# Seven-product pairs of the up projection: sums by accumulation in PSUM, and 19 pairs instead of 16

## The chip, the cores and the metric

The kernel runs on one core of one Trainium2 chip. The metric is the device time of one execution in microseconds (us); lower is better. Six engines matter here: TensorE (PE in the profile, with its weight loads as PEld), VectorE (DVE), ScalarE (ACT), GpSimd (POOL) and the DMA queues, of which SyncE (SP) issues most.

## What is computed

The reference is one decoder layer on 512 tokens of width 1024: adaLN modulation, a token mixer, a residual with LayerNorm, then a convolutional gated MLP and a second residual with LayerNorm. Only the MLP is touched:

```
def conv_ffn(h, w_up, conv_w, conv_b, w_down):
    u = causal_dwconv(h @ w_up, conv_w, conv_b)
    g, val = jnp.split(u, 2, axis=-1)
    return (jax.nn.silu(g) * val) @ w_down
```

`w_up` is 1024 x 5632 (g and val, 2816 columns each), `w_down` 2816 x 1024, all float32. The depthwise convolution has three taps along the tokens.

## The kernel before

Every float32 operand is split into a high and a low part of the type fp32r, and a product is three matmuls (high by high, high by low, low by high; `mm3`, line 456). Splitting is a copy by ScalarE (the high part, `wh` or the first half of `wq`) and a subtraction by VectorE (the low part).

The up projection has 22 pairs: pair j is 128 columns of g and the 128 columns of val that are multiplied with them. A plain pair is two tiles of 8 row chunks of 128: 2 x 8 x 3 = 48 matmuls of 128x128 weights by 512 tokens, into two banks of PSUM. Pairs 0 and 1 run in two halves of the tokens. A pair in the list `SEVEN` (line 695) is computed in Winograd's form of Strassen's scheme: the pair's weights (g and val columns, rows 0 to 511 and 512 to 1023) and the activations (the same rows, tokens 0 to 255 and 256 to 511) are 2 x 2 blocks, and seven products of sums of blocks take the place of eight. Each product is 4 chunks x 3 = 12 matmuls by 256 tokens, so a pair is 84.

- `sums_seven` (line 716) forms two sums of weight blocks by DMA: one load by SP and two accumulating DMAs by POOL per pair.
- `split_seven` (line 764) forms two more sums on VectorE (`sw`) and splits the seven left operands into `wq`: seven copies on ScalarE, seven subtractions on VectorE.
- `quarters` (line 1318) forms and splits four sums of activation blocks, `ts`, once.
- `seven` (line 1660) issues the products 0, 1, 2, 4, 5, 6, 3 into four banks, `sP`. `seven_out` (line 1692) combines them: two ScalarE copies to SBUF (`m1`) and seven VectorE additions of 256 columns.
- `up_post` (line 1358) then does, for each of the two tiles, the convolution: one ScalarE pass and two VectorE passes (`conv3`); after that a Silu, the product of the two tiles, and for j below 6 the split of the result (`mid`); the others are kept and split later.

The down projection (`dn`) follows, 122.76 us of TensorE.

The order of instructions is written by a planner in the kernel's own code (class `Order`): coroutines offer their next operation, the planner prices it, keeps a clock per engine, and issues what could start first, by priority among those close together. Once written, the order is fixed: each engine takes its instructions in that order and waits by semaphores. Pools bound what may be ahead: 8 banks of PSUM, 9 buffers `s` (2 KB a partition: `sw`, `m1`, `u2`, `u`), 10 buffers for split weights in this stage. In the trace all operations have line 309, where the planner issues them; they are told apart by tiles.

Of the kernel before, what the change touches and what calls it, by code (L numbers as in the profile page):

```python
# [11 lines left out]
AF = mybir.ActivationFunctionType  # L12
# [4 lines left out]
P = 128  # L17
# [396 lines left out]
def layer_kernel(  # L414
# [21 lines left out]
    R = Order(nc)  # L436
    T, V, A, G, S, GD = (Engine(R, k) for k in ("PE", "V", "A", "G", "S", "GD"))
# [15 lines left out]
    def row_bc(src, off, n):  # L453
        return bass.AP(tensor=src.tensor, offset=src.offset + off, ap=[[0, P], [1, n]])

    def mm3(ps, lh, ll, rh, rl, start, stop):
        return [T.matmul(ps, lh, rh, start=start, stop=False),
                T.matmul(ps, lh, rl, start=False, stop=False),
                T.matmul(ps, ll, rh, start=False, stop=stop)]

    def bank(group, name="ps", after=()):
        return Alloc("ps", [P, 512], F32, name, group, after)

    def buf(cls, shape, name, group=None, dt=F32):
        return Alloc(cls, shape, dt, name, group)
# [226 lines left out]
            rows_item(w_out, k, n)  # L692
    UP0 = len(items)
    NSPLIT = 4
    SEVEN = [3, 5, 6, 7, 8, 10, 11, 12, 13, 15, 16, 17, 18, 19, 20, 21]
    for j, i in up_tiles:
        cols_item(w_up, i * D_FF + j * P)
    for n in range(2):
# [4 lines left out]
    def w_load():  # L703
        yield Need("loads")
        for i, (shape, src) in enumerate(items):
# [4 lines left out]
            j = (i - UP0) // 2  # L710
            if i == UP0 + 2 * j + 1 and j in SEVEN:
                R.spawn(sums_seven(j, raw, items[i - 1][1][:, :4], src[:, :4]), 4)
# [3 lines left out]
    def sums_seven(j, r1, a11, a21):  # L716

        q = yield buf("s", [P, 4, P], "sw")
        yield S.dma_start(q, a11)
        yield GD.dma_start(r1[:, :4], r1[:, 4:], accum_op=OP.add)  # L720
        yield GD.dma_start(q, a21, accum_op=OP.add)
        QS[j] = q
        R.mark(("qs", j))

    def w_split():
        yield Need(("hk", KC - 1))
        for i, (shape, _) in enumerate(items):
# [6 lines left out]
            if 0 <= i - len(items) + LATE_DN < 2:  # L734
                yield Need("fin")
                m = 2 * (i - len(items) + LATE_DN)
                hi, lo = RES["w"][:, m], RES["w"][:, m + 1]
            elif UP0 <= i < UP0 + 2 * NFF and (i - UP0) // 2 in SEVEN:
                if (i - UP0) % 2 == 0:
# [24 lines left out]
    def split_seven(j, r0, r1):  # L764

        yield Need(("qs", j))
        a11, a12, s1, a22, s3 = r0[:, :4], r0[:, 4:], r1[:, :4], r1[:, 4:], QS.pop(j)
        dst, src, tmp = {}, {0: a11, 1: s1, 4: s3, 5: a12, 6: a22}, {}

        def make(m, x, y):  # L770
            t = tmp[m] = yield buf("s", [P, 4, P], "sw")
            yield V.tensor_add(t, x, y)
            src[m] = t

        def hi(m):
            dst[m] = yield buf("b", [P, 2, 4, P], "wq", "w2", F32R)
            yield A.activation(dst[m][:, 0], src[m], AF.Copy)

        def lo(m):
            q = [dst[m][:, 1], src[m], dst[m][:, 0].bitcast(F32)]  # L780
            yield V.tensor_sub(*q)
            WS[j, m] = dst[m]
            lead[1] += 2 / 7
            R.mark(("ws", j, m))

        yield from hi(0)
        yield from hi(1)
        yield from make(2, s1, a11)
        yield from lo(0)
        yield from lo(1)  # L790
        yield from hi(2)
        yield from lo(2)
        yield from hi(4)
        yield from make(3, src[2], a12)
        R.free(tmp[2])
        yield from lo(4)
        R.free(s3)
        for m in (5, 6, 3):
            yield from hi(m)
            yield from lo(m)  # L800
        R.free(tmp[3])

    def w_next():
        i = wpos[0]
        wpos[0] += 1
        if not (UP0 <= i < UP0 + 2 * NFF and (i - UP0) // 2 in SEVEN):
            lead[0] += 1
        R.mark(("item", i))
        return ("w", i), i
# [541 lines left out]
    def conv3(ps, dst, ch, neg):  # L1351
        f0, f1, f2 = (nfw[:, i, ch - NFF:ch - NFF + 1] if neg else w[:, ch:ch + 1] for i, w in enumerate((fw0, fw1, fw2)))
        yield A.activation(dst, ps, AF.Identity, bias=fb[:, ch:ch + 1], scale=f2)
        for s, fw in ((1, f1), (2, f0)):
            yield V.scalar_tensor_tensor(dst[:, s:], ps[:, :SEQ - s], fw, dst[:, s:], op0=OP.mult, op1=OP.add)
        R.free(ps)

    def up_post(j, i, ps, neg=False):
        u = yield buf("s", [P, SEQ], "u")
        yield from conv3(ps, u, j + 22 * i, neg)  # L1360
        if i == 0:
            yield A.activation(u, u, AF.Silu)
            U[j] = u
            R.mark(("u", j))
            return
        yield Need(("u", j))
        g = U.pop(j)
        if j >= NMID:
            if not 12 <= j < 20 and j % 2 == 0:
                KEEP[j] = yield buf("b", [P, 2, SEQ], "keep", "mid")  # L1370
                R.mark(("keep", j))
            n = 4 if 12 <= j < 20 else 2
            yield Need(("keep", j - j % n))
            k = KEPT[j] = KEEP[j - j % n][:, j % n]
            yield V.tensor_mul(k, g, u)
            R.free(g, u)
            R.mark(("kept", j))
            return
        yield V.tensor_mul(g, g, u)
        R.free(u)  # L1380
        mid = yield buf("b", [P, 2, SEQ], "mid", "mid", F32R)
        yield A.activation(mid[:, 0], g, AF.Copy)
        yield V.tensor_sub(mid[:, 1], g, mid[:, 0].bitcast(F32))
        R.free(g)
        MID[j] = mid
        R.mark(("mid", j))
# [109 lines left out]
    def products():  # L1496
# [37 lines left out]
        for kind, i in G1:  # L1534
            if kind == "v":
# [3 lines left out]
                for k0 in range(0, KC, 2):  # L1539
                    key, n = w_next()  # L1540
                    yield Need(key)
                    hi, lo = W.pop(n)
                    for kk in range(2):
                        k = k0 + kk
                        for t in range(NT):
                            yield mm3(ps[t], hh[:, k, t * P:(t + 1) * P], hl[:, k, t * P:(t + 1) * P],
                                      hi[:, kk], lo[:, kk], k == 0, k == KC - 1)
                    R.free(hi, lo)
# [3 lines left out]
            else:  # L1552
# [4 lines left out]
                for k in range(KC):  # L1557
                    yield mm3(ps, w[0][:, k], w[1][:, k], hh[:, k], hl[:, k], k == 0, k == KC - 1)
# [99 lines left out]
    L, H = slice(0, 256), slice(256, 512)  # L1658

    def seven(j):  # L1660

        h2h, h2l = H2["hl"]
        for _ in range(2):
            w_next()
        ps = []
        for i in range(2):
            ps.append((yield bank("gemm", "sP")))

        def b(k0, c):
            return h2h[:, k0:k0 + 4, c], h2l[:, k0:k0 + 4, c]  # L1670

        def t(m):
            return TS[m][:, 0], TS[m][:, 1]

        yield Need("ts")
        R.mark("tsused")

        for m, p, c, (rh, rl) in ((0, 0, L, b(0, L)), (1, 1, L, t(0)), (2, 0, H, t(1)), (4, 1, H, t(2)),
                                  (5, 2, L, b(4, L)), (6, 3, L, t(3)), (3, 2, H, b(4, H))):
            if p == len(ps):  # L1680
                ps.append((yield bank("gemm", "sP")))
            yield Need(("ws", j, m))
            w = WS.pop((j, m))
            lead[0] += 2 / 7
            for k in range(4):
                yield mm3(ps[p][:, c], w[:, 0, k], w[:, 1, k], rh[:, k], rl[:, k], k == 0, k == 3)
            R.free(w)
            if m == 0:
                R.spawn(seven_out(j, ps), 2)
            R.mark(("sm", j, m))  # L1690

    def seven_out(j, ps):
        m1 = yield buf("s", [P, 2, 256], "m1")
        yield A.activation(m1[:, 0], ps[0][:, L], AF.Copy)
        yield Need(("sm", j, 1))
        yield A.activation(m1[:, 1], ps[1][:, L], AF.Copy)
        yield Need(("sm", j, 2))
        u2 = yield buf("s", [P, 2, 256], "u2")
        yield V.tensor_add(u2[:, 0], ps[0][:, H], m1[:, 0])
        R.free(ps[0])  # L1700
        yield Need(("sm", j, 4))
        yield V.tensor_add(u2[:, 1], ps[1][:, H], u2[:, 0])
        R.free(ps[1])
        yield Need(("sm", j, 5))
        yield V.tensor_add(ps[2][:, L], ps[2][:, L], m1[:, 0])
        yield V.tensor_add(u2[:, 0], u2[:, 0], m1[:, 1])
        yield Need(("sm", j, 6))
        yield V.tensor_add(ps[3][:, L], ps[3][:, L], u2[:, 1])
        yield V.tensor_add(ps[3][:, H], u2[:, 1], m1[:, 1])
        R.free(m1)  # L1710
        R.spawn(up_post(j, 1, ps[3], True), 2)
        yield Need(("sm", j, 3))
        yield V.tensor_add(ps[2][:, H], ps[2][:, H], u2[:, 0])
        R.free(u2)
        R.spawn(up_post(j, 0, ps[2]), 2)

    def ffn():
        h2h, h2l = H2["hl"]
# [21 lines left out]
        for n, (j, i) in enumerate(up_tiles[NSPLIT:]):  # L1740
            if j in SEVEN:
                if i == 0:
# [115 lines left out]
```

## Time and profile before

| | |
|---|---|
| median of 3 runs | 704.72 us (703.95 to 705.64) |
| profiled execution | 704.55 us, span 702.5 us |
| PE busy | 688.8 us of the span (98%) |
| DVE busy | 621.0 us (88%) |
| ACT busy | 367.0 us (52%) |
| granted TensorE clock, mean | 0.997 |
| up projection, first to last matmul | 343.9 to 572.3 us |
| down projection on PE | 572.28 us, for 122.76 us |

Busy time is the time in which at least one instruction of the engine is running; instructions of an engine overlap somewhat, so the distance between the starts of successive instructions is often shorter than the duration shown. An idle time has the name of what ended it. A granted clock of 1.00 is 2.4 GHz.

### The profile page before, as it was taken

What the parts mean: (1) busy time and instruction counts of PE and PEld (TensorE: products, weight loads), DVE (VectorE), ACT (ScalarE), POOL (GpSimd) and SP (SyncE); (2) the same over time, 40 slices, a digit from 0 to 9 for tenths busy, and PEclk for the clock granted to TensorE, in tenths of its full rate; (3) what the DMA queues carried; (4) which work ended last, traced back from release to release, by engine and by line L of the source; (5) the groups of instructions that cost most, each with busy time, mean ns of one, the idle gap of its engine ahead of it and who ended that gap; (6) DMA issues with size and microseconds to landing.
All of it is one profiled execution on the core that took longest, in us unless ns stands there. A gap on an engine that the chain in (4) does not pass through costs nothing.

```text
span 702.5 us, 11338 instructions
## 1 busy us (share of the span) xinstructions
PE 688.8 (98%) x4197; PEld 595.4 (85%) x4197; DVE 621.0 (88%) x1172; ACT 367.0 (52%) x680; POOL 97.2 (14%) x103
## 2 busy tenths in 40 slices
PE   8999999999999999999999999999999999999995
PEld 7787777888888888887898899899899998888885
DVE  5889989899999999889999999999999999567646
ACT  2447568846677454223886556656655676211300
POOL 0010021101000000000111112112111100960023
PEclk9999999999999999999999999999999999999998
DMA  8997074143455727776576466766777574432202
GB/s 268 315 281 249 5 235 127 37 117 98 122 182 169 235 68 253 254 265 216 171 184 141 109 162 166 150 162 176 142 193 154 136 248 167 156 103 76 91 30 91
DMA packets 131322, 114.25 MB, mean 163 GB/s; under 512 B 4421, under 2 KB 110273, under 8 KB 131267
## 3 DMA queue, kind: packets, MB, share of 16 engines
q1 hardware_dynamic: 120515, 105.14, 48.4%
q0 software_dynamic: 10752, 8.39, 8.4%
q8 instruction: 33, 0.54, 0.3%
q14 instruction: 22, 0.18, 0.1%
HBM read 105.09 MB, written 4.23 MB: 156 GB/s over the span
## 4 chain that ended last, share of the span: by engine, by line
PE 83%; DVE 8%; DMA 3%; SPq 3%; issue 1%; ACT 1%; POOL 0%; DVEq 0%; ACTq 0%; POOLq 0%
PE sP L309 20%; PE fm L309 18%; PE dn L309 17%; PE po L309 7%; PE up L309 6%; PE first L309 3%; SPq L309 3%; PE tm L309 2%; DVE u L309 2%; DVE wq L309 2%; PE psS L309 2%; PE pov L309 1%; PE pT L309 1%; PE py L309 1%; DMA csb<-drcs 1%
## 5 line engine op out<-in xcount | busy, mean ns | idle before, releaser
L309 DVE TENSOR_TENSOR wl<-raw,wh 128x1024 fp32r<-128x1024 f32 x70 | 87.2, 1250 | 25.8 <-ACT wh L309 25.6
L309 ACT ACTIVATE wh<-raw 128x1024 fp32r<-128x1024 f32 x70 | 73.4, 1054 | 69.1 <-DVE raw L309 23.3
L309 PE MATMUL dn<-wh,mid 128*128 128x512 f32 (+1 forms) x356 | 102.6, 371 | 0.0
L309 PE MATMUL sP<-ts,wq 128*128 128x256 f32 x768 | 96.1, 281 | 0.0
L309 PEld LDWEIGHTS sP<-ts,wq 128*128 128x128 f32 x768 | 92.9, 188 | 0.2 <-ACT m L309 0.2
L309 PEld LDWEIGHTS dn<-wh,mid 128*128 128x128 f32 x356 | 64.6, 188 | 12.6
L309 PE MATMUL sP<-h2h,wq 128*128 128x256 f32 x384 | 74.4, 282 | 0.0
L309 PE MATMUL fm<-hh,wh 128*128 128x512 f32 x176 | 72.6, 412 | 0.0
L309 PE MATMUL fm<-hh,wl 128*128 128x512 f32 x176 | 69.4, 394 | 0.0
L309 PE MATMUL fm<-hl,wh 128*128 128x512 f32 x176 | 69.4, 394 | 0.0
L309 PE MATMUL dn<-wl,mid 128*128 128x512 f32 (+1 forms) x178 | 66.1, 371 | 0.0
L309 PEld LDWEIGHTS sP<-h2h,wq 128*128 128x128 f32 x384 | 61.6, 189 | 0.5 <-DVE sP L309 0.3
L309 PE MATMUL sP<-h2l,wq 128*128 128x256 f32 x192 | 53.9, 281 | 0.0
L309 DVE TENSOR_TENSOR wq<-raw,wq 128x512 fp32r<-128x512 f32 x64 | 43.1, 685 | 0.2
L309 PE MATMUL up<-h2h,wh 128*128 128x256 f32 (+1 forms) x128 | 43.2, 338 | 0.0
L309 PE MATMUL up<-h2l,wh 128*128 128x256 f32 (+1 forms) x128 | 43.2, 337 | 0.0
L309 PE MATMUL up<-h2h,wl 128*128 128x256 f32 (+1 forms) x128 | 43.1, 337 | 0.0
L309 PE MATMUL po<-wh,os 128*128 128x512 f32 x128 | 42.1, 396 | 0.0
L309 PEld LDWEIGHTS fm<-hh,wl 128*128 128x128 f32 x176 | 33.1, 188 | 7.7
L309 ACT ACTIVATE wq<-raw 128x512 fp32r<-128x512 f32 x64 | 37.6, 621 | 3.6 <-DVE u L309 2.1
L309 PEld LDWEIGHTS fm<-hh,wh 128*128 128x128 f32 x176 | 33.2, 188 | 7.1 <-issue 0.7
L309 PEld LDWEIGHTS dn<-wl,mid 128*128 128x128 f32 x178 | 33.5, 188 | 6.2
(268 smaller groups left out, 1540.5 us busy)
## 6 DMA issues: line engine op xcount, KB each, us to landing
raw<-in_ffn_up_w_dram SPq DMA_DIRECT2D x44, 512.0 KB, 3.9
raw<-in_mix_in_w_dram SPq DMA_DIRECT2D x26, 512.0 KB, 5.5
ad<-in_ada_w_dram SPq DMA_DIRECT2D x24, 512.0 KB, 4.0
raw<-in_ffn_down_w_dram SPq DMA_DIRECT2D x22, 512.0 KB, 4.1
aw<-in_ada_w_dram SPq DMA_DIRECT2D x32, 256.0 KB, 5.8
raw<-in_mix_out_w_dram SPq DMA_DIRECT2D x12, 512.0 KB, 4.0
csb<-drcs SPq DMA_DIRECT2D x8, 512.0 KB
ad<-in_ada_w_dram SPq DMA_DIRECT2D x4, 1024.0 KB
```

The lines of the kernel that those rows point to most:

```text
L309: getattr(self.hw[op.eng], op.fn)(*op.args, **op.kw)
```

## The change

`SEVEN` now holds the pairs 3 to 21, 19 of them; pair 2 alone remains plain, and pairs 4, 9 and 14 pass from plain to seven products. Within a pair, products are added up in PSUM where their sum is wanted: product 0 opens an accumulation in the left half of the first bank, products 2, 4 and 6 go on in it, and product 3 goes on in product 1's half of the second bank. Because other results need the partial sums, ScalarE copies the half to SBUF (`c1`, `c2`) after products 0, 2, 1 and 4; products 2, 4, 3 and 6 start only after the copy of what they add to (`Need(("sc", j, after))`). Two VectorE additions are left of seven, one of 512 columns and one of 256. A pair takes two banks instead of four. The products run in the order 0, 5, 2, 1, 4, 3, 6, and the weights are split in the order 0, 5, 2, 1, 4, 3, 6. `seven_out` has priority 1 instead of 2.

```diff
-    SEVEN = [3, 5, 6, 7, 8, 10, 11, 12, 13, 15, 16, 17, 18, 19, 20, 21]
+    SEVEN = list(range(3, 22))
...
         yield from hi(0)
-        yield from hi(1)
+        yield from hi(5)
         yield from make(2, s1, a11)
         yield from lo(0)
-        yield from lo(1)
+        yield from lo(5)
         yield from hi(2)
         yield from lo(2)
-        yield from hi(4)
+        yield from hi(1)
         yield from make(3, src[2], a12)
         R.free(tmp[2])
-        yield from lo(4)
-        R.free(s3)
-        for m in (5, 6, 3):
+        yield from lo(1)
+        for m in (4, 3, 6):
...
-        for m, p, c, (rh, rl) in ((0, 0, L, b(0, L)), (1, 1, L, t(0)), (2, 0, H, t(1)), (4, 1, H, t(2)),
-                                  (5, 2, L, b(4, L)), (6, 3, L, t(3)), (3, 2, H, b(4, H))):
-            if p == len(ps):
-                ps.append((yield bank("gemm", "sP")))
+        for m, p, c, (rh, rl), after, go_on in ((0, 0, L, b(0, L), None, True), (5, 1, L, b(4, L), None, False),
+                                                (2, 0, L, t(1), 0, True), (1, 1, H, t(0), None, True),
+                                                (4, 0, L, t(2), 2, True), (3, 1, H, b(4, H), 1, False),
+                                                (6, 0, L, t(3), 4, False)):
+            if after is not None:
+                yield Need(("sc", j, after))
...
-                yield mm3(ps[p][:, c], w[:, 0, k], w[:, 1, k], rh[:, k], rl[:, k], k == 0, k == 3)
+                yield mm3(ps[p][:, c], w[:, 0, k], w[:, 1, k], rh[:, k], rl[:, k],
+                          k == 0 and after is None, k == 3 and not go_on, p == 0 or m in (1, 3))
...
     def seven_out(j, ps):
-        m1 = yield buf("s", [P, 2, 256], "m1")
-        yield A.activation(m1[:, 0], ps[0][:, L], AF.Copy)
...
+        c1 = yield buf("s", [P, 2, 256], "c1")
+        yield A.activation(c1[:, 0], ps[0][:, L], AF.Copy)
+        R.mark(("sc", j, 0))
+        c2 = yield buf("s", [P, 2, 256], "c2")
+        yield Need(("sm", j, 2))
+        yield A.activation(c1[:, 1], ps[0][:, L], AF.Copy)
+        R.mark(("sc", j, 2))
+        yield Need(("sm", j, 1))
+        yield A.activation(c2[:, 0], ps[1][:, H], AF.Copy)
+        R.mark(("sc", j, 1))
         yield Need(("sm", j, 4))
+        yield A.activation(c2[:, 1], ps[0][:, L], AF.Copy)
+        R.mark(("sc", j, 4))
+        yield Need(("sm", j, 3))
+        yield V.tensor_add(ps[1], ps[1], c1)
+        R.free(c1)
+        R.spawn(up_post(j, 0, ps[1]), 2)
         yield Need(("sm", j, 6))
+        yield V.tensor_add(ps[0][:, H], c2[:, 0], c2[:, 1])
+        R.free(c2)
+        R.spawn(up_post(j, 1, ps[0], True), 2)
```

The planner writes the order anew from pair 3 on. On TensorE, around products 1, 2 and 4 of pair 3, it was this (`sP_3888` and `sP_3889` are the first two banks, `ts_3588` to `ts_3590` the activation sums, `wq` the split weights):

```order
L309 MATMUL sP_3888<-h2l_2830,wq_3795 128x256
L309 MATMUL sP_3888<-h2h_2829,wq_3795 128x256
L309 MATMUL sP_3889<-ts_3588,wq_3800 128x256 x12
L309 MATMUL sP_3888<-ts_3589,wq_3842 128x256 x12
L309 MATMUL sP_3889<-ts_3590,wq_3849 128x256 x12
L309 MATMUL sP_3985<-h2h_2829,wq_3858 128x256
```

and is now, in the two banks `sP_3892` and `sP_3893`:

```order
L309 MATMUL sP_3893<-h2l_2830,wq_3804 128x256
L309 MATMUL sP_3893<-h2h_2829,wq_3804 128x256
L309 MATMUL sP_3892<-ts_3589,wq_3846 128x256 x12
L309 MATMUL sP_3893<-ts_3588,wq_3853 128x256 x12
L309 MATMUL sP_3892<-ts_3590,wq_3862 128x256 x12
L309 MATMUL sP_3893<-h2h_2829,wq_3880 128x256
```

The products alternate between the two banks, so one product of 12 matmuls lies between a product and the next that adds to it; a third bank is not taken.

On ScalarE, at the change from one pair to the next late in the stage, the order before was this (`u` from `sP` is the convolution's first pass, `u` from `u` the Silu, `m` the copies of `seven_out`, `wq` from `raw` or `sw` the weights of the next pair):

```order
L309 ACTIVATE u_5533<-sP_5506,fprm_91,nfw_92 128x512
L309 ACTIVATE u_5550<-sP_5488,fprm_91 128x512
L309 ACTIVATE m_1097_5562<-sP_5544 128x256
L309 ACTIVATE wq_5564<-sw_5499 128x512
L309 ACTIVATE wq_5581<-raw_5302 128x512
L309 ACTIVATE m_1097_5562<-sP_5545 128x256
L309 ACTIVATE wq_5591<-raw_5424 128x512
L309 ACTIVATE u_5550<-u_5550 128x512
L309 ACTIVATE wq_5630<-sw_5601 128x512
L309 ACTIVATE wq_5647<-sw_5427 128x512
L309 ACTIVATE wq_5669<-raw_5302 128x512
```

and is now, in a piece that repeats with every late pair (`c_1151` is `c1`, `c_1153` is `c2`):

```order
L309 ACTIVATE u_5952<-sP_5823,fprm_91 128x512
L309 ACTIVATE u_5972<-sP_5822,fprm_91,nfw_92 128x512
L309 ACTIVATE c_1151_5981<-sP_5959 128x256
L309 ACTIVATE wq_5986<-raw_5731 128x512
L309 ACTIVATE wq_6004<-raw_5733 128x512
L309 ACTIVATE u_5952<-u_5952 128x512
L309 ACTIVATE wq_6013<-raw_5733 128x512
L309 ACTIVATE c_1151_5981<-sP_5959 128x256
L309 ACTIVATE wq_6044<-sw_6023 128x512
L309 ACTIVATE c_1153_5988<-sP_5960 128x256
L309 ACTIVATE c_1153_5988<-sP_5959 128x256
```

Four copies stand in a pair's piece where two stood; the second stands behind a Silu, and the third behind a weight copy that reads a sum by VectorE (`sw_6023`).

On VectorE the additions of one pair stood among the weight subtractions like this (`u_1106` is the buffer `u2`):

```order
L309 TENSOR_TENSOR u_1106_5609<-sP_5544,m_1097_5562 128x256
L309 TENSOR_TENSOR u_1106_5609<-sP_5545,u_1106_5609 128x256
L309 TENSOR_TENSOR sw_5649<-sw_5601,raw_5302 128x512
L309 TENSOR_TENSOR wq_5647<-sw_5427,wq_5647 128x512
L309 TENSOR_TENSOR wq_5669<-raw_5302,wq_5669 128x512
L309 TENSOR_TENSOR sP_5625<-sP_5625,m_1097_5562 128x256
L309 TENSOR_TENSOR u_1106_5609<-u_1106_5609,m_1097_5562 128x256
L309 TENSOR_TENSOR sP_5642<-sP_5642,u_1106_5609 128x256
L309 TENSOR_TENSOR wq_5680<-raw_5424,wq_5680 128x512
L309 TENSOR_TENSOR sP_5642<-u_1106_5609,m_1097_5562 128x256
L309 TENSOR_TENSOR sP_5625<-sP_5625,u_1106_5609 128x256
L309 TENSOR_TENSOR wq_5699<-sw_5649,wq_5699 128x512
```

and now stand like this, with the convolution's passes behind them (`c_1129` is `c1`, `c_1131` is `c2`):

```order
L309 TENSOR_TENSOR wq_5929<-raw_5731,wq_5929 128x512
L309 TENSOR_TENSOR sP_5823<-sP_5823,c_1129_5844 128x512
L309 TENSOR_TENSOR wq_5946<-sw_5734,wq_5946 128x512
L309 TENSOR_TENSOR sP_5822<-c_1131_5851 128x256
L309 SCALAR_TENSOR_TENSOR u_5952<-sP_5823,fprm_90,u_5952 128x511
L309 TENSOR_TENSOR wq_5962<-sw_5934,wq_5962 128x512
L309 SCALAR_TENSOR_TENSOR u_5952<-sP_5823,fprm_90,u_5952 128x510
L309 TENSOR_TENSOR wq_5986<-raw_5731,wq_5986 128x512
L309 SCALAR_TENSOR_TENSOR u_5972<-sP_5822,nfw_92,u_5972 128x511
L309 TENSOR_TENSOR sw_6023<-raw_5868,raw_5733 128x512
L309 TENSOR_TENSOR wq_6004<-raw_5733,wq_6004 128x512
L309 TENSOR_TENSOR wq_6013<-raw_5733,wq_6013 128x512
```

Seven additions became two. A late pair on VectorE is now 16 instructions and nothing else: 9 of 512 columns for the weights, 2 additions, 4 convolution passes and one product.

## Rows read from the trace of the kernel before

**Rows 1.** The page, part 1: busy us, share of span, instructions of each engine.
```profile
PE 688.8 (98%) x4197; PEld 595.4 (85%) x4197; DVE 621.0 (88%) x1172; ACT 367.0 (52%) x680; POOL 97.2 (14%) x103
```

**Rows 2.** Chain that ended last, 409 to 695 us: start us, us, engine and tile.
```profile
409.30 31.46 PE sP L309 x264
440.76 11.08 PE up L309 x48
451.84 39.81 PE sP L309 x336
491.65 11.19 PE up L309 x48
502.84 69.44 PE sP L309 x588
572.28 122.76 PE dn L309 x594
```

**Rows 3.** Windows: stretch, length, busy us of PE, PEld, DVE, ACT, POOL, clock, DMA.
```profile
441.00:452.00 11.00, 11.00 (x50) 8.97 (x50) 10.81 (x20) 6.21 (x11) 0.87 (x1) 1.00 0.67 152
452.00:470.00 18.00, 18.00 (x153) 18.00 (x152) 17.75 (x34) 11.41 (x21) 3.45 (x3) 1.00 0.67 134
...
590.00:600.00 10.00, 10.00 (x44) 8.08 (x44) 8.21 (x12) 5.69 (x10) 2.23 (x2) 1.00 0.83 293
```

**Rows 4.** Waits of TensorE's weight loads, 343 to 573 us: total, times, longest.
```profile
PEld pad L309 <- DVE accl L309: 0.4, 1, 0.4
PEld sP L309 <- DVE sP L309: 0.3, 1, 0.3
PEld sP L309 <- ACT m L309: 0.2, 1, 0.2
```

**Rows 5.** Timeline of VectorE, 546 to 549 us: start us, us, engine, operation, tiles.
```profile
546.04 0.43 DVE L309 TENSOR_TENSOR sP<-sP,u 128x256 f32<-128x256 f32 x1
546.37 0.69 DVE L309 TENSOR_TENSOR sw<-raw,raw 128x512 f32<-128x512 f32 x1
546.97 0.69 DVE L309 TENSOR_TENSOR wq<-raw,wq 128x512 fp32r<-128x512 f32 x1
547.57 0.75 DVE L309 SCALAR_TENSOR_TENSOR u<-sP,fprm,u 128x511 f32<-128x511 f32 x1
548.23 0.68 DVE L309 TENSOR_TENSOR wq<-raw,wq 128x512 fp32r<-128x512 f32 x1
```

**Rows 6.** Page part 5, VectorE's split of a plain weight block: busy, mean ns.
```profile
L309 DVE TENSOR_TENSOR wl<-raw,wh 128x1024 fp32r<-128x1024 f32 x70 | 87.2, 1250 | 25.8 <-ACT wh L309 25.6
```

**Rows 7.** Tile sP: duration ns min/median/max, first and last start us, forms.
```profile
L309 ACT ACTIVATE m<-sP x32: 358/385/388, 381.9 to 565.2; 128x256 f32<-128x256 f32 x32
...
L309 DVE TENSOR_TENSOR sP<-sP,u x32: 424/428/434, 388.9 to 576.4; 128x256 f32<-128x256 f32 x32
```

**Rows 8.** Timeline of TensorE and ScalarE after product 0 of pair 17.
```profile
523.97 4.35 PE L309 MATMUL sP<-ts,wq 128*128 128x256 f32 x36
524.23 0.39 ACT L309 ACTIVATE m<-sP 128x256 f32<-128x256 f32 x1 [1.69 <-PE sP L309]
```

**Rows 9.** The same after product 0 of pair 3: TensorE, then ScalarE.
```profile
380.75 4.68 PE L309 MATMUL sP<-ts,wq 128*128 128x256 f32 x36
...
381.91 0.83 ACT L309 ACTIVATE m<-sP 128x256 f32<-128x256 f32 x2
```

**Rows 10.** The same after product 0 of pair 12.
```profile
472.80 0.78 ACT L309 ACTIVATE u<-sP,fprm,nfw 128x512 f32<-128x512 f32 x1 [4.16 <-DVE sP L309]
...
476.00 0.39 ACT L309 ACTIVATE m<-sP 128x256 f32<-128x256 f32 x1 [0.19 <-PE sP L309]
...
473.03 4.35 PE L309 MATMUL sP<-ts,wq 128*128 128x256 f32 x36
```

**Rows 11.** DMA issues, 343 to 573 us: count, KB each, median us to landing.
```profile
raw<-raw POOLq DMA_DIRECT2D x16, 256.0 KB, 4.5
sw<-in_ffn_up_w_dram POOLq DMA_DIRECT2D x16, 256.0 KB, 5.2
```

More of the change, by code (lines that the diff above doesn't have):

```diff
@@ L454, in row_bc, with mm3 @@
         return bass.AP(tensor=src.tensor, offset=src.offset + off, ap=[[0, P], [1, n]])
[L456 to L459, printed above, removed]
+    def mm3(ps, lh, ll, rh, rl, start, stop, part=False):
+        return [T.matmul(ps, lh, rh, start=start, stop=False, skip_group_check=part),
+                T.matmul(ps, lh, rl, start=False, stop=False, skip_group_check=part),
+                T.matmul(ps, ll, rh, start=False, stop=stop, skip_group_check=part)]
     def bank(group, name="ps", after=()):
@@ L786, in split_seven @@
         yield from hi(0)
-        yield from hi(1)
+        yield from hi(5)
         yield from make(2, s1, a11)
         yield from lo(0)
-        yield from lo(1)
+        yield from lo(5)
         yield from hi(2)
         yield from lo(2)
-        yield from hi(4)
+        yield from hi(1)
         yield from make(3, src[2], a12)
         R.free(tmp[2])
-        yield from lo(4)
-        R.free(s3)
-        for m in (5, 6, 3):
+        yield from lo(1)
+        for m in (4, 3, 6):
             yield from hi(m)
             yield from lo(m)
-        R.free(tmp[3])
+            if m in tmp:
+                R.free(tmp[m])
+        R.free(s3)
     def w_next():
@@ L1685, in seven @@
             for k in range(4):
-                yield mm3(ps[p][:, c], w[:, 0, k], w[:, 1, k], rh[:, k], rl[:, k], k == 0, k == 3)
+                yield mm3(ps[p][:, c], w[:, 0, k], w[:, 1, k], rh[:, k], rl[:, k],
+                          k == 0 and after is None, k == 3 and not go_on, p == 0 or m in (1, 3))
             R.free(w)
             if m == 0:
-                R.spawn(seven_out(j, ps), 2)
+                R.spawn(seven_out(j, ps), 1)
             R.mark(("sm", j, m))
     def seven_out(j, ps):
-        m1 = yield buf("s", [P, 2, 256], "m1")
@@ L1694, in seven_out @@
-        yield A.activation(m1[:, 0], ps[0][:, L], AF.Copy)
-        yield Need(("sm", j, 1))
[L1696 to L1700, printed above, removed]
-        yield Need(("sm", j, 4))
[L1702 to L1705, printed above, removed]
@@ L1706, in seven_out @@
-        yield V.tensor_add(u2[:, 0], u2[:, 0], m1[:, 1])
-        yield Need(("sm", j, 6))
[L1708 to L1715, printed above, removed]
+        c1 = yield buf("s", [P, 2, 256], "c1")
+        yield A.activation(c1[:, 0], ps[0][:, L], AF.Copy)
```

## The prediction

> **What bounds the kernel now.** I read the page's busy times first. TensorE is busy 688.8 us of a span of 702.5, VectorE 621.0, ScalarE 367.0 [rows 1]: the reader is to see one engine without room and a second that is close behind. That is an average, so the chain of waits comes next. From 409 us to the end of the down projection it is TensorE without a break [rows 2]: four stretches of the up projection in turn, narrow ones (`sP`, products of 256 columns) and wide ones (`up`, plain pairs of 512), then `dn`. So in the stage that is changed a microsecond less of matmuls is a microsecond less of time, as long as nothing else takes the place. The table of windows says what stands closest [rows 3]: in a narrow stretch VectorE is busy 17.75 us of 18, ScalarE 11.41, and the DMA engines 0.67 of the time; the clock is granted in full, 1.00, the 2.4 GHz level. VectorE leaves free time only after the stage, 8.21 us of 10 at 590 us. It works off a backlog until then. TensorE nevertheless hardly waits: in all of 343 to 573 us the waits of its weight loads are three, 0.9 us together [rows 4].
>
> **The pace of the two forms.** The three narrow stretches are 31.46 + 39.81 + 69.44 = 140.71 us for 264 + 336 + 588 = 1188 matmuls [rows 2]: 118.4 ns each, 84 x 118.4 = 9.95 us for a pair by seven products. The two wide ones are 22.27 us for 96: 232.0 ns each, 48 x 232.0 = 11.13 us for a plain pair. A pair that changes its form is 1.18 us shorter on TensorE, and three do (4, 9 and 14): **-3.6 us**. All of it is on the chain.
>
> The Trainium skill has a rule by which this would be a loss: "TensorE: Matmul & The Clock Gate", section "Back-to-back issue gap", gives a stream of weight loads and matmuls as about 81 ns at 128 columns and 131 ns at 512. Between them I estimate, by a straight line from that page, 98 ns at 256; a pair would be 84 x 98 = 8.2 us by seven products and 48 x 131 = 6.3 us plain, and three pairs would cost 5.8 us. This trace disagrees, with 232 ns at 512 columns and 118 at 256.
>
> **VectorE.** Of a pair by seven products it did seven additions of 256 columns, and now does one of 512 and one of 256. I take the distance between starts as the price, since an instruction starts before the one ahead of it has ended [rows 5]: 0.33 us for an addition of 256 columns (546.04 to 546.37), 0.60 for one of 512 (546.37 to 546.97), 0.66 for a convolution pass (547.57 to 548.23). No row shows a 512-column addition in PSUM; at 256 columns one there takes 0.43 us [rows 7], as the first of rows 5 does, so I take 0.60. A pair was 9 x 0.60 for the weights + 7 x 0.33 + 4 x 0.66 + 0.60 for the product of its tiles = 10.95 us, and becomes 9 x 0.60 + 0.60 + 0.33 + 4 x 0.66 + 0.60 = 9.57. A plain pair has two splits of 1.25 us at most [rows 6] and 3.24 us of the rest: 5.7. Over pairs 2 to 21 that is 16 x 10.95 + 4 x 5.7 = 198 us before, and 19 x 9.57 + 5.7 = 188 us after, against 16 x 9.95 + 4 x 11.13 = 204 us of TensorE before and 200 after. So before, one narrow pair asked for 1.0 us more of VectorE than of TensorE, and the plain pairs in between paid it back; now a narrow pair asks for 0.4 less, and none need come between. That is what makes three more narrow pairs in a row possible. By itself it saves no time: VectorE was behind TensorE's edge before too. If the price were the duration shown instead (0.69, 0.43, 0.75 us in rows 5), a pair would be 9 x 0.69 + 0.69 + 0.43 + 4 x 0.75 + 0.69 = 11.0 us, 1.05 more than TensorE has; the starts exclude most of that, and I keep it as a rival.
>
> **The new waits of TensorE.** This is the one cost that the trace does not show: products 2, 4, 3 and 6 wait for a copy, 4 x 19 = 76 times. Between a product and the next that adds to it lies one other product, 12 x 118.4 ns = 1.42 us. After product 0 of pair 17 the next product starts at 523.97 and the copy at 524.23 [rows 8], so a copy starts 0.26 us after the product; it lasts 0.385 us [rows 7]; for the way back I take the same 0.26. Sum 0.91 of 1.42: the wait costs nothing, and the cover is 0.5 us. A copy that starts later than 0.26 + 0.5 = 0.77 us after its product stops TensorE. ScalarE takes its instructions in order, and behind a copy that is late stand the next pair's weights. Of the 32 copies before [rows 7] I laid against their products those that could be laid; two pairs had a late one: pair 3, at 381.91 against 380.75 [rows 9], 1.16 us, and pair 12, at 476.00 against 473.03 [rows 10], 2.97 us, behind a convolution pass that had waited 4.16 us for VectorE. Under the new order they would have cost 1.16 + 0.385 + 0.26 - 1.42 = 0.39 and 2.20 us. 2.6 us on 32 copies is 6.2 us on 76: the upper bound. The lower bound is a gain: the 0.9 us of waits in this stage could go [rows 4]. I take **+0.6 us**, two waits of the size of rows 4's second, in the pairs 3 to 5, where VectorE still has the residual's work and pairs 0 and 1 to clear. Two things put the value near the lower end: nothing waited for these copies before, so the planner put them at 476 us behind both convolution passes of the pair before, and gives them more priority now; and a VectorE at 9.57 of 9.95 us does not fall behind by 4 us from pair to pair.
>
> **What rides along.** ScalarE does two more copies a pair, 0.77 us on 9.95, about 8% on top of 11.41 of 18 us [rows 3]: covered while the copies themselves are on time, which is the term above. Three pairs more bring six POOL DMAs and three loads by SP. A sum lands 4.5 and 5.2 us after its issue [rows 11], and is wanted a pair later, after 9.95 us; the DMA engines are two thirds busy [rows 3]. Behind them on POOL stand only the sums of the next pair. I cost them at nothing; if the cover went, the first product that reads a sum would wait the rest of the 5.2 us. A pair needs two banks and not four, so VectorE may be up to four pairs late before TensorE lacks a bank. The new order of the weights follows the new order of the products and costs nothing. `dn` starts earlier by what the stage saves and keeps its 122.76 us [rows 2], since VectorE then has less left over than before.
>
> **The sum.** The profiled execution took 704.55 us, 0.17 below the median of its runs, so no correction. 704.55 - 3.6 + 0.6 = **701.6 us**.
>
> **The rivals.**
> - *The copies block (slower).* A copy stands behind a Silu or a weight copy that waits for VectorE, starts over 0.77 us late, and TensorE stops; the place is the second and third copy of each pair. For it: the order on ScalarE, and the 4.16 us of rows 10. Against it: a copy that starts 0.26 us after the product [rows 8], and VectorE's new room. At the upper bound 704.55 - 3.6 + 6.2 = 707.2 us.
> - *VectorE becomes the bound.* In 18 narrow pairs that follow each other it cancels the gain once a pair asks for 3.6 / 18 = 0.2 us more than TensorE's 9.95, that is 0.6 over my sum. For it: 17.75 of 18 us busy, and additions that must wait for products 3 and 6 in its order. Against it: a pair is 1.4 us lighter than before. With 0.15 us over per pair, 704.55 - 3.6 + 2.7 + 0.6 = 704.2 us. At the durations, 1.05 us per pair, it would be 19 us slower, which the starts exclude.
> - *The narrow form does not pay.* The weight loads are busy 18.00 of 18 us in a narrow stretch and 8.97 of 11 in the wide one [rows 3], so a narrow matmul has its load as its pace. At the slowest pace in the rows, 36 matmuls in 4.68 us [rows 9], 130 ns, a pair is 10.9 us, the three pairs save 0.6, and the time is 704.5 us. Against it: 1188 matmuls at 118.4 ns. The rule of the Trainium skill named above would go further, into a loss.
>
> **How the numbers follow.** About 0.2%, 1.4 us, is what a measurement of this kernel can tell from no change: faster is below 703.3 us, slower above 706.1. My forecast gets 0.72, VectorE as the bound 0.14, blocked copies 0.11, the narrow pace 0.03. Faster: 0.72 and a fifth of VectorE's case, 0.75. Slower: most of the blocked copies, 0.08, and 0.01 of VectorE's. The same: the rest, 0.16. The range begins at 700.1 (the 0.9 us of waits gone and none added is 704.55 - 3.6 - 0.9) and reaches to 704.6, which takes in the narrow pace and the smaller part of VectorE's case, and leaves the blocked copies out.
>
> **What would show it.** Right: a narrow pair still near 9.95 us; from 411 us on one narrow stretch without a wide one, no wait of TensorE over 0.5 us, and those few before pair 6; the copies starting 0.2 to 0.3 us after their products; VectorE with short idle times in every pair, where it had none; `dn` beginning near 569 us, 122.8 us long. Wrong: waits of TensorE for `c1` or `c2` in pair after pair (the copies), or idle times of ScalarE before convolution passes that grow from pair to pair with VectorE at no idle (VectorE), or a narrow pair of over 10.9 us with no wait in it (the pace).

## The result, and the profile after

The changed kernel takes 700.36 us (median of 4 runs, 699.56 to 700.99); the kernel before, run beside it, 705.18 us (703.95 to 706.08). The ratio is 0.9932, with a 95% interval of 0.9919 to 0.9945: 4.8 us less, at least 3.9. The forecast was 701.6 us in a range of 700.1 to 704.6, so the sign was right and the time lies in the range, with a gain 1.2 us larger than forecast. The profiled execution of the changed kernel took 700.32 us, 4.23 below the profiled one of before, and the sections below compare these two.

The page, part 1, of the changed kernel (busy us, share of the span, instructions), to be read against [rows 1]:

```profile
PE 684.3 (98%) x4305; PEld 598.0 (86%) x4305; DVE 607.3 (87%) x1119; ACT 387.8 (56%) x739; POOL 103.4 (15%) x109
```

TensorE has 108 matmuls more (three pairs with 84 in place of 48) and is busy 4.5 us less. VectorE is 13.7 us lighter, ScalarE 20.8 heavier. The end of the chain that ended last (start us, us, engine and tile), against [rows 2]:

```profile
380.76 187.56 PE sP L309 x1587
568.32 122.87 PE dn L309 x594
```

Where before three narrow stretches alternated with wide ones, one narrow stretch runs from pair 3 to the down projection: 187.56 / 1587 = 118.2 ns for a matmul, 9.93 us for a pair. `dn` begins 3.96 us earlier than in [rows 2] and is within 0.11 us as long as it was. The span from the first to the last instruction is 4.0 us shorter (698.5 against 702.5). The other 0.23 us of the 4.23 lie outside the span: there the kernel before has 2.0 to 2.1 us in every run whose span is on record, and the changed kernel 1.7 to 1.8. No row shows what they are. The waits of TensorE's weight loads from 343 to 573 us (total, times, longest), against [rows 4]:

```profile
PEld pad L309 <- DVE accl L309: 0.4, 1, 0.4
```

This is the old wait of `pad`. None of the 76 new waits for a copy shows, and the two waits of `sP` in [rows 4] are gone. Tile `sP` in the changed kernel (duration ns min/median/max, first and last start, forms), against [rows 7]:

```profile
L309 ACT ACTIVATE c<-sP x76: 363/384/387, 381.3 to 565.5; 128x256 f32<-128x256 f32 x76
...
L309 DVE TENSOR_TENSOR sP<-sP,c x19: 676/694/700, 388.9 to 566.9; 128x512 f32<-128x512 f32 x19
...
L309 DVE TENSOR_TENSOR sP<-c x19: 414/433/434, 390.1 to 568.4; 128x256 f32<-128x256 f32 x19
```

The copies take what they took; the sum of 512 columns that had no row before takes 0.69 us as other additions of that size do. One pair in ScalarE's timeline (start us, us, tiles, idle time before it and its releaser):

```profile
510.26 0.38 ACT L309 ACTIVATE c<-sP 128x256 f32<-128x256 f32 x1 [0.22 <-PE sP L309]
...
513.03 0.39 ACT L309 ACTIVATE c<-sP 128x256 f32<-128x256 f32 x1 [0.31 <-PE sP L309]
...
514.47 0.38 ACT L309 ACTIVATE c<-sP 128x256 f32<-128x256 f32 x1 [0.53 <-PE sP L309]
...
515.86 0.39 ACT L309 ACTIVATE c<-sP 128x256 f32<-128x256 f32 x1 [1.00 <-PE sP L309]
```

All four were released by TensorE: ScalarE stood ready, up to 1.00 us early, and the copies start 0.2 to 0.26 us after their products (the last of them 0.20 us after TensorE went on at 515.66). Over all pairs 56 of the 76 copies were released so; the other 20 stood behind other work of ScalarE, but none so late that TensorE waited. The windows (length, busy us of PE, PEld, DVE, ACT, POOL, clock, DMA), against [rows 3]:

```profile
452.00:470.00 18.00, 18.00 (x154) 18.00 (x153) 17.85 (x30) 12.84 (x26) 3.48 (x3) 1.00 0.79 166
...
590.00:600.00 10.00, 10.00 (x45) 8.07 (x44) 2.96 (x2) 2.12 (x2) 9.77 (x8) 1.00 0.33 107
```

In a narrow stretch VectorE looks as full as before, 17.85 of 18 us; at 590 us it has 2.96 us of work left in 10, where it had 8.21. Read alone, the first line would say that VectorE has no room. What a pair asks of it had to be measured in another way, below.

### The profile page after: what moved, and what is told of

The parts are those of the page before. It is cut to its first block, busy times and chain, and to the rows that moved or that the text cites. A ratio compares the mean times of both kernels' runs of the same rounds, so it can differ in the third digit from the quotient of the medians.

```text
span 698.5 us, 11597 instructions
## 1 busy us (share of the span) xinstructions
PE 684.3 (98%) x4305; PEld 598.0 (86%) x4305; DVE 607.3 (87%) x1119; ACT 387.8 (56%) x739; POOL 103.4 (15%) x109
## 3 DMA queue, kind: packets, MB, share of 16 engines
HBM read 106.66 MB, written 4.23 MB: 159 GB/s over the span
## 4 chain that ended last, share of the span: by engine, by line
PE 85%; DVE 6%; DMA 4%; SPq 3%; ACT 1%; issue 1%; POOL 0%; DVEq 0%; ACTq 0%; POOLq 0%
PE sP L309 27%; PE fm L309 18%; PE dn L309 18%; PE po L309 7%; PE first L309 3%; SPq L309 3%; PE tm L309 2%; PE psS L309 2%; PE pov L309 1%; PE pT L309 1%; PE py L309 1%; DMA csb<-drcs 1%; PE pyo L309 1%; PE up L309 1%; DMA raw<-in_ffn_up_w_dram 1%
## 5 line engine op out<-in xcount | busy, mean ns | idle before, releaser
L309 PE MATMUL sP<-ts,wq 128*128 128x256 f32 x912 | 113.9, 281 | 0.0
L309 PEld LDWEIGHTS sP<-ts,wq 128*128 128x128 f32 x912 | 110.4, 189 | 0.0
L309 PE MATMUL sP<-h2h,wq 128*128 128x256 f32 x456 | 87.2, 281 | 0.0
L309 PEld LDWEIGHTS sP<-h2h,wq 128*128 128x128 f32 x456 | 72.7, 189 | 0.0
L309 PE MATMUL sP<-h2l,wq 128*128 128x256 f32 x228 | 64.0, 281 | 0.0
L309 DVE TENSOR_TENSOR wq<-raw,wq 128x512 fp32r<-128x512 f32 x76 | 50.8, 686 | 0.7
L309 ACT ACTIVATE wq<-raw 128x512 fp32r<-128x512 f32 x76 | 45.3, 623 | 0.0
L309 ACT ACTIVATE c<-sP 128x256 f32<-128x256 f32 x76 | 29.0, 382 | 28.5 <-PE sP L309 28.2
L309 PEld LDWEIGHTS sP<-h2l,wq 128*128 128x128 f32 x228 | 43.1, 189 | 0.1
L309 DVE TENSOR_TENSOR wq<-sw,wq 128x512 fp32r<-128x512 f32 x57 | 38.8, 684 | 0.0
```

Of the source, the lines that this page charges most:

```text
L309: getattr(self.hw[op.eng], op.fn)(*op.args, **op.kw)
```

## The experiments

My theory after the result: the gain is the three pairs at 1.18 us each, the copies are free because a product lies between, and VectorE's lighter share gives no time itself but lets narrow pairs follow each other. The rivals: the lighter VectorE or the accumulation is itself the gain; the list alone would have done it; the copies are on time only by their priority.

**The accumulation with the old list.**

```diff
-    SEVEN = list(range(3, 22))
+    SEVEN = [3, 5, 6, 7, 8, 10, 11, 12, 13, 15, 16, 17, 18, 19, 20, 21]
```

> The changed code with the old list of 16 narrow pairs: pairs 4, 9 and 14 are wide again. Theory (the list alone gives the gain, 1.18 us for a pair; accumulation and its waits cost and give nothing by themselves): the changed kernel's 700.4 us + 3.6 = 704.0, at most the 0.9 us of waits of TensorE that are gone below the kernel before (704.3 to 705.2); TensorE from the first narrow pair to dn takes 224.0 + 3.6 = 227.6 us, against 228.2 before. Rival (the lighter VectorE is itself the gain, by waits that no row names): below 702.5 us. Second rival (the 64 new waits cost, and the three pairs give more than 1.18 each): above 706 us.

Measured: 703.56 us (8 runs), ratio to before 0.9975 (0.9965 to 0.9985). The end of its chain:

```profile
491.42 11.15 PE up L309 x48
502.57 69.51 PE sP L309 x588
572.08 122.54 PE dn L309 x594
```

The stretches are those of [rows 2] to 0.1 us, and `dn` begins at 572.08 against 572.28. So of the 3.96 us by which `dn` came earlier, 3.76 belong to the list and 0.20 to the accumulation. The medians say 3.2 us for the list and 1.7 (1.1 to 2.5) for the accumulation; the profiled run of this kernel is at the top of its own runs, 703.76. The list is the larger part either way, and both rivals are out. The accumulation alone gives some 0.8 us by the profiled runs (703.76 against 704.55) and more by the medians, more than the 0.9 us bound that I set. Half of the 0.8 lies outside the span (1.66 us against 2.05). In the stage, the two waits of `sP` in [rows 4], 0.5 us together, are gone, and one new wait for a copy, 0.2 us, has come. What gives the rest of the 1.7 us, no row names; it stays open.

**The old sums with 18 narrow pairs in a row.**

```diff
 (kernel before)
-    SEVEN = [3, 5, 6, 7, 8, 10, 11, 12, 13, 15, 16, 17, 18, 19, 20, 21]
+    SEVEN = [4, 5, 6, 7, 8, 9, 10, 11, 12, 13, 14, 15, 16, 17, 18, 19, 20, 21]
```

> The kernel before, with its seven additions a pair, but 18 narrow pairs in a row (4 to 21). The planner finds no order for 19 under the old scheme. Theory (VectorE sets the limit of narrow pairs in a row: 10.95 us a pair against 9.95 of TensorE): TensorE has 18 x 9.95 + 11.13 from pair 3 on, 1.18 x 2 = 2.4 us less than before; VectorE comes 1 us further behind with each pair, and waits of TensorE in the later pairs, for weights or for a bank, take back all of it and more: 705 to 713 us. Rival (TensorE alone sets the time, the accumulation was not needed for it): 705.2 - 2.4 = 702.8 us, with no wait of TensorE over 0.5 us.

Measured: 718.26 us, ratio 1.0183 (1.0169 to 1.0197), 13 us slower than before and above the theory's 713. The chain repeats itself from pair to pair:

```profile
484.14 3.10 PE sP L309 x24
487.54 1.16 ACT wq L309 x2
488.70 1.27 DVE wq L309 x2
...
494.74 0.76 DVE u L309
495.63 3.11 PE sP L309 x24
```

TensorE comes into it with 24 matmuls of 84 and ScalarE with two weight copies, 1.16 us; nearly all the rest is VectorE. A pair takes 495.63 - 484.14 = 11.49 us, and the windows (as above) show who is full in it:

```profile
484.14:495.63 11.49, 10.17 (x84) 9.99 (x85) 11.35 (x22) 6.59 (x12) 2.16 (x2) 1.00 0.75 163
```

VectorE 11.35 of 11.49 us, TensorE 10.17. TensorE stands 1.3 us before product 0 of each of the last ten pairs. Its matmul waits for VectorE's convolution pass, which can only be for the bank that the pass reads; its weight load waits for ScalarE's weight copy, which ends within 0.1 us of that pass and stands behind convolution passes that waited for VectorE. So 18 narrow pairs in a row without the accumulation are a loss, and VectorE is what forbids them. It asks 11.5 us, not the 10.95 that I had summed. Some of its timeline (start us, us) shows why:

```profile
499.25 0.42 DVE L309 TENSOR_TENSOR u<-sP,m 128x256 f32<-128x256 f32 x1
499.58 0.68 DVE L309 TENSOR_TENSOR sw<-raw,raw 128x512 f32<-128x512 f32 x1
...
502.99 0.42 DVE L309 TENSOR_TENSOR sP<-sP,u 128x256 f32<-128x256 f32 x1
503.44 0.43 DVE L309 TENSOR_TENSOR sP<-u,m 128x256 f32<-128x256 f32 x1
503.91 0.69 DVE L309 TENSOR_TENSOR sw<-sw,raw 128x512 f32<-128x512 f32 x1
...
505.46 1.52 DVE L309 SCALAR_TENSOR_TENSOR u<-sP,nfw,u 128x511 f32<-128x511 f32 x2
506.90 0.74 DVE L309 SCALAR_TENSOR_TENSOR u<-sP,fprm,u 128x511 f32<-128x511 f32 x1
```

The addition at 499.25 costs 0.33 us to the next start, as I had it. Those at 502.99 and 503.44, on the two halves of one bank, cost 0.45 and 0.47; why, no row tells. The two convolution passes at 505.46, of which the second continues what the first wrote, cost (506.90 - 505.46) / 2 = 0.72 each, where I took 0.66 from a row with another instruction in between.

**No product between a copy and the product that waits for it.**

```diff
-        for m, p, c, (rh, rl), after, go_on in ((0, 0, L, b(0, L), None, True), (5, 1, L, b(4, L), None, False),
+        for m, p, c, (rh, rl), after, go_on in ((5, 1, L, b(4, L), None, False), (0, 0, L, b(0, L), None, True),
```

> The changed kernel with product 5 ahead of product 0, so that product 2, which waits for the copy of product 0, comes right behind product 0; the other three waits keep one product of 1.42 us as their cover. Theory (the copies cost nothing because that product hides 0.26 + 0.385 + 0.26 = 0.91 us): each pair shows one wait of TensorE of 0.8 to 1.0 us for ScalarE's copy, 19 x 0.9 = 17 us, so 715 to 719 us. Rival (a wait for a copy costs little even without cover, since TensorE's weight loads run ahead or the copy starts earlier than I read): below 704 us.

Measured: 713.85 us, 13.5 above the changed kernel. Its waits of weight loads for a copy:

```profile
PEld sP L309 <- ACT c L309: 12.9, 19, 0.7
```

One wait a pair, 12.9 us in sum, as the theory has it, but 0.68 us each and not 0.9. The timeline gives the parts (TensorE, then ScalarE):

```profile
499.47 0.28 PE L309 MATMUL sP<-h2h,wq 128*128 128x256 f32 x1
500.22 4.50 PE L309 MATMUL sP<-ts,wq 128*128 128x256 f32 x36 [0.47 <-ACT c L309]
...
499.78 0.38 ACT L309 ACTIVATE c<-sP 128x256 f32<-128x256 f32 x1 [0.26 <-PE sP L309]
```

The last matmul of product 0 starts at 499.47, so at a pace of 0.118 us another could have started at 499.59. The copy starts 0.19 later, lasts 0.38 to 500.16, and product 2 starts 0.06 after that: 0.63 us in all. Of the cover of 1.42 us, 0.79 are left, where I had counted 0.5.

**The copies' priority.**

```diff
-                R.spawn(seven_out(j, ps), 1)
+                R.spawn(seven_out(j, ps), 2)
```

> The changed kernel with the priority that the copies and sums had before (2 instead of 1, equal to that of the Silu and the last product). Theory (copies are on time because VectorE is no longer late, and the priority adds nothing): within 0.5 us of the changed kernel's 700.4. Rival (the priority is what keeps the copies on time): waits of TensorE for c1 or c2, some us slower, 702 to 706.

Measured: 699.97 us (699.22 to 701.29), ratio 0.9925 (0.9911 to 0.994), the changed kernel's within the interval, and again `pad` is the only wait of weight loads. The priority shows no effect.

**More work for VectorE.** One addition that nothing reads, then two:

```diff
         yield V.tensor_add(ps[1], ps[1], c1)
+        yield V.tensor_add(c1, c1, c1)
```

> The changed kernel with one more addition of 512 columns on VectorE in each narrow pair (c1 + c1 into c1, which nothing reads any more). Theory (VectorE asks 9.57 us a pair by the distances between starts, so 0.36 us a pair are free): 9.57 + 0.60 = 10.17 us asked against 9.93 of TensorE, 0.24 x 19 = 4.6 us behind by the last pair, part of which the weights split ahead take up: 700.4 to 705. Rival (VectorE has nothing left, as its 168.62 of 170 us busy suggest): 0.5 to 0.6 us for each pair, 19 x 0.55 = 10 us, 709 to 712.

> The changed kernel with two more additions of 512 columns on VectorE in each narrow pair. Theory (0.36 us free a pair): 9.57 + 1.20 = 10.77 us asked, 0.84 x 19 = 16 us behind less what the weights split ahead take up: 711 to 717, and VectorE without idle time sets the length of every pair. Rival (nothing left): 1.15 x 19 = 22 us, 720 to 723.

With one: 705.05 us, 4.7 above the changed kernel, ratio to before 1.0002 (0.9991 to 1.0013). One addition a pair spends the whole gain. Its chain and a part of VectorE's timeline:

```profile
509.65 0.71 DVE c L309
...
515.67 1.21 DVE wq L309 x2
...
518.83 0.75 DVE u L309
...
520.22 0.70 DVE c L309
```

```profile
530.07 0.69 DVE L309 TENSOR_TENSOR sP<-sP,c 128x512 f32<-128x512 f32 x1
530.79 0.69 DVE L309 TENSOR_TENSOR c<-c 128x512 f32<-128x512 f32 x1
531.52 0.69 DVE L309 TENSOR_TENSOR sw<-sw,raw 128x512 f32<-128x512 f32 x1
```

VectorE now sets the pace: 520.22 - 509.65 = 10.57 us a pair. The added instruction costs 0.73, and the one ahead, whose operand `c` it overwrites, 0.72 in place of 0.60. Without both the pair would ask 10.57 - 0.73 - 0.12 = 9.72 us. So I estimate that the changed kernel leaves VectorE 0.2 us of 9.93, not the 0.36 of the expectation, and not nothing, as 17.85 of 18 us busy suggested.

How a late VectorE reaches TensorE is in the waits of its weight loads, and in ScalarE's and TensorE's timelines:

```profile
PEld sP L309 <- ACT c L309: 4.3, 8, 0.6
```

```profile
532.33 0.78 ACT L309 ACTIVATE u<-sP,fprm 128x512 f32<-128x512 f32 x1 [2.44 <-DVE sw L309]
...
534.05 0.37 ACT L309 ACTIVATE c<-sP 128x256 f32<-128x256 f32 x1
...
534.47 4.56 PE L309 MATMUL sP<-ts,wq 128*128 128x256 f32 x36 [0.35 <-ACT c L309]
```

A convolution pass on ScalarE waits 2.44 us for VectorE; behind it stand weight copies and then the copy, which comes too late for product 2. These eight waits, seven of them one a pair from 492 us on, are 4.3 of the 4.7 us. Before that only one wait shows, at 402 us; that work done ahead took up VectorE's lag until then fits, but is not shown. The time came out at the theory's upper end, and the rival's 709 did not, but the match is luck: VectorE asked 10.57 us and not 10.17, and TensorE paid for it in seven or eight pairs and not in all 19.

With two: 726.42 us, beyond both theories. Here a third thing came in, to be seen in the windows from 490 us and in TensorE's timeline:

```profile
490.00:492.00 2.00, 0.00 (x0) 0.00 (x0) 1.86 (x4) 0.70 (x2) 0.00 (x0) 1.00 0.05 9
492.00:494.00 2.00, 1.35 (x9) 1.35 (x10) 2.00 (x4) 1.64 (x4) 0.00 (x0) 0.88 0.04 8
494.00:496.00 2.00, 2.00 (x12) 2.00 (x11) 2.00 (x4) 1.42 (x3) 0.00 (x0) 0.50 0.38 110
496.00:498.00 2.00, 2.00 (x15) 2.00 (x15) 0.87 (x2) 0.94 (x3) 0.48 (x1) 0.77 0.07 21
```

```profile
492.65 4.38 PE L309 MATMUL sP<-ts,wq 128*128 128x256 f32 x22 [2.91 <-DVE wq L309]
```

TensorE stood 2.91 us for a weight split (after a stand of 0.84 us at 487 us), and the granted clock then fell to 0.50, the 1.2 GHz level: 22 matmuls took 4.38 us, 199 ns each in place of 118. The stands of 1.3 us in the run with the old sums left the clock at 1.00. Both numbers of the theories left the clock out, and so this run says nothing about the free 0.2 us.

**Longer copies.** Each copy twice, then three times:

```diff
         yield A.activation(c1[:, 0], ps[0][:, L], AF.Copy)
+        yield A.activation(c1[:, 0], ps[0][:, L], AF.Copy)
```

(and so at the other three)

> The changed kernel with each copy of a partial sum done twice, the same into the same place, before the next product may start: 0.29 us later. Theory (cover 1.42 us; the copy was back 0.68 to 0.91 us after its product, by the run with product 5 first and by my sum, and is now 0.97 to 1.2): no wait, within 1 us of 700.4. Rival (the waits were close to showing): 76 x 0.05 us and more, from 704 us on.

> The changed kernel with each copy of a partial sum done three times before the next product may start: 0.58 us later. Theory A (the copy is back 0.68 us after its product, as the wait with product 5 first was 0.68 us long): 0.68 + 0.58 = 1.26 of 1.42 us of cover, few waits, 700.4 to 702. Theory B (back after 0.91 us, the sum of the prediction): 1.49 of 1.42, 0.07 us at each of 76 places, 5 us, 704 to 707. With either, ScalarE has 4 x 0.58 = 2.3 us more a pair on about 7.3 of 9.93, so that rests of its own may come on top.

Twice: 701.33 us, ratio 0.9944 (0.9929 to 0.996), one wait of 0.4 us for `c`. That is theory, within 1 us of 700.36. ScalarE's timeline shows what a doubled copy takes:

```profile
511.60 0.79 ACT L309 ACTIVATE c<-sP 128x256 f32<-128x256 f32 x2
```

That is 0.40 us more than one copy of 0.385, not the 0.29 that I had expected: so much longer a copy may take. Three times: 720.86 us, far from either theory, so it doesn't tell 0.68 from 0.91. The windows, the waits of weight loads and ScalarE's timeline show what happened in its place:

```profile
440.00:520.00 80.00, 76.64 (x610) 73.04 (x610) 71.70 (x116) 71.01 (x161) 15.32 (x14) 1.00 0.73 161
```

```profile
PEld sP L309 <- ACT c L309: 14.9, 36, 0.8
```

```profile
503.20 0.77 ACT L309 ACTIVATE u<-sP,fprm,nfw 128x512 f32<-128x512 f32 x1
503.86 1.15 ACT L309 ACTIVATE wq<-raw 128x512 fp32r<-128x512 f32 x2
504.90 2.32 ACT L309 ACTIVATE c<-sP 128x256 f32<-128x256 f32 x6
```

ScalarE, which takes its instructions in the order written, is busy 71.01 of 80 us; the copies of two products stand one behind the other, after the weights and passes ahead of them. Copies that no longer find ScalarE ready do block TensorE, 36 times, 14.9 of the 20.5 us. So the rival *the copies block* is a real mechanism: it comes in when ScalarE has too much to do, and, in the run with one more addition, when a pass ahead of the copy waits for VectorE. The changed kernel, with ScalarE busy 12.84 us of 18, shows neither; where the border lies between that and 71.01 of 80, no run shows.

**One more narrow pair.** With pair 2 in the list too, the last adaptive row (`ada_last`) gets another priority: 4 in the first run; in the second, shown here, 1, but only from the seventh weight load of the stage on.

```diff
-    SEVEN = list(range(3, 22))
+    SEVEN = list(range(2, 22))
...
-    R.spawn(ada_last(), 8)
+    R.spawn(ada_last(), lambda: 8 if ('item', UP0 + 6) not in R.done else 1)
```

> The changed kernel with pair 2 by seven products too (20 narrow pairs), and the last adaptive row given priority 4 instead of 8, without which the planner finds no order. Theory (a pair by seven products is worth 1.18 us wherever its weights are in time): 700.4 - 1.2 = 699.2 us. Rival (the weights or the tile sums of pair 2 come too late, as pair 3 already shows waits at 380 us): a new wait of 1 us or more before 380 us, 700.4 us or slower.

> 20 narrow pairs as in the run before with 20, but the last adaptive row gets its priority (1) only when the seventh of the up projection's weight loads is done, so that the stage before is left as in the changed kernel. Theory (the 20 pairs gave 1.2 us in their own stage, 346.04 to 568.83 = 222.8 us against 224.0, and the early row lost 0.6 ahead of it): up stage 222.8 us long, 699.2 us. Rival (pair 2 as a narrow pair makes waits that moved to the stage before): 699.8 us or slower.

The first: 699.81 us, ratio 0.9926 (0.9913 to 0.9938), not to be told from the changed kernel: its stage is 1.2 us shorter, but begins at 346.04 us, 1.7 later than the changed kernel's 344.32, behind a wait of 1.9 us of the transposes `pt` for VectorE. The second: **697.64 us**, ratio 0.9899 (0.9884 to 0.9914), faster than both kernels. Its chain:

```profile
343.77 6.34 PE up L309 x54
...
381.66 184.28 PE sP L309 x1566
565.94 122.58 PE dn L309 x594
```

The stage lasts 565.94 - 343.77 = 222.2 us, 1.8 less than the changed kernel's 224.0 (568.32 - 344.32): more than the 1.2 of one pair. The pace in it is 184.28 / 1566 = 117.7 ns, 0.5 below the changed kernel's, which over 1680 matmuls is 0.8 us. The rival that pair 2 loses it all again is out. What sets the last half nanosecond I didn't try.

## Why the prediction was right, step by step

- **The pace of the two forms: right.** 118.4 ns became 118.2, a pair 9.93 us where I had 9.95, and the list alone moved `dn` by 3.76 us in the profiled runs and the time by 3.2 in the medians, for a term of -3.6. The rule of the Trainium skill that would have made it a loss ("TensorE: Matmul & The Clock Gate", section "Back-to-back issue gap") does not hold here either: the estimate from it was 5.8 us lost by the three pairs, and the list gained 3.2.
- **The new waits of TensorE: mis-sized.** The term was +0.6 us; it measured 0, and the two waits of `sP` in [rows 4], 0.5 us, went as well. By these rows that is nearly the whole difference between 701.6 and 700.36. It is not the whole account: the medians give the accumulation by itself a gain of 1.7 us (1.1 to 2.5), where the prediction had only this cost for it, and the list 3.2 in place of 3.6. Some 0.4 us of the 1.7 lie outside the span, and the rest beyond the waits stays open. Two assumptions stood behind the +0.6. The way back was taken to be as long as the way there, 0.26 us; it is 0.06. And late copies, as in [rows 9, 10], were expected in the first pairs; none was late enough to show. The reason that I gave for the second, a VectorE that no longer falls behind, holds; the run with one more addition shows the other side, a VectorE that falls behind and copies that come late by it. The other reason, more priority, was idle: the run with the old priority has the same time.
- **VectorE: right in what it decides, low in size.** I summed 10.95 us a pair before and 9.57 after; the runs in which VectorE sets the pace show 11.5 and, without the added work, 9.72. The distances between starts in [rows 5] are those between neighbours that have nothing to do with each other. A pass that continues what its neighbour wrote costs 0.72 in place of 0.66, and the additions on one bank 0.45 in place of 0.33. So the room is some 0.2 us a pair, half of what I had, and the rival *VectorE becomes the bound* was nearer than its 0.14 said: one addition a pair, 0.85 us with what it costs its neighbour, took back the whole gain. The prediction kept this rival apart from *the copies block*; the waits of that run show that a late VectorE reaches TensorE through a late copy. That 18 narrow pairs in a row pay only with the lighter VectorE is shown by the run with the old sums, 718.26 us.
- **What rides along: right.** The DMA engines went from 0.67 to 0.79 in the narrow windows, ScalarE from 11.41 to 12.84 of 18 us, and no weight load waits for a weight. `dn` begins at 568.32 us, near the 569 named, and is 122.87 long.
- **What would show it.** Four signs came as named: one narrow stretch, a pair near 9.95 us, no wait over 0.5, and copies that start 0.2 to 0.26 us after their products. One did not: VectorE shows hardly more idle time than before, 17.85 of 18 us busy. Its durations overlap the next start, so that 0.2 us of room cannot be read there.

## What to carry to other kernels

When a form that is faster on the bound engine costs another engine more, sum what each form asks of that second engine, and test the sum by making it the bound: the old sums with 18 narrow pairs lost 13 us, the new sums with 19 gained 5. A wait inside a stream cost nothing here while enough other work of the same engine lay between cause and effect; take its parts from rows (0.19 + 0.38 + 0.06 us, against 1.42 of cover), and see that the engine that answers it stands ready, and that nothing ahead of the answer waits for a third engine. Price a VectorE instruction twice, between neighbours that are independent and right behind the one that it depends on.

## What the runs showed of the hardware that was not expected

- From the end of a ScalarE copy to the matmul that waited for it passed 0.06 us; the copy itself had started 0.19 us after the time at which another matmul could have followed its product's last one (500.16 to 500.22 and 499.59 to 499.78 in the run without cover).
- On VectorE the next instruction starts 0.60 us after an addition of 512 columns [rows 5], but 0.72 after one whose operand it overwrites (530.07 to 530.79 in the run with one more addition); after a convolution pass 0.66 [rows 5], but 0.72 if it continues that pass's output (505.46 to 506.90, two passes, in the run with the old sums). The one behind such an instruction was late too: 0.73 us from 530.79 to 531.52, though it does not touch `c`.
- After TensorE had stood 2.91 us (and 0.84 us shortly before), the granted clock was 0.88 and then 0.50 in the next two windows of 2 us that were read; it stayed at 1.00 with a stand of 1.3 us in each pair of the run with the old sums.
